# An adding transfer in place of every second low-part subtraction in layer 1's MLP

## The chip, the cores and the metric

The kernel runs on one core of a Trainium2 chip. The metric is the device time of one execution in microseconds; lower is better. Engines are named by their work: TensorE (PE in the profile, PEld for its weight loads), VectorE (DVE), ScalarE (ACT), GpSimd (POOL) and SyncE (SP, which here only issues loads). Transfers run on the core's sixteen DMA engines, whichever engine issues them.

## The reference, cut to what matters

Two encoder layers on 256 tokens of width 2048, in float32. Each layer has attention and then an MLP; only the MLP matters here.

```python
D_MODEL = 2048; SEQ = 256; D_FF = 4 * D_MODEL
for l in range(2):
    ...                                     # modulation, attention, residual
    h = _rmsnorm(x) * (1.0 + sc_m) + sh_m   # (256, 2048)
    y = jnp.square(jax.nn.relu(h @ w_mlp_in[l])) @ w_mlp_out[l]
    x = x + g_m * y
return _rmsnorm(x, final_norm_g)
```

The first product is `h @ w_mlp_in[l]`, 2048 x 8192 weights; the second is the one with `w_mlp_out[l]`, 8192 x 2048.

## The kernel before, in words

**Products in parts.** TensorE multiplies in a shortened format (`F32R`). For float32 accuracy every operand v is split into a high part, v rounded to that format, and a low part, v minus the high part. A product is then three: high by high, high by low and low by high. Where the 256 tokens are the moving operand, one matmul of 512 columns (high and low part of the tokens side by side) takes the weight's high part (line 217), and one of 256 columns the weight's low part (line 220).

**Weights on their way.** `weights(src)` loads one tile of 128 x 2048 float32 (1024 KB) into a buffer of the tag `raw`, of which there are five, by SP's queue (line 170). `part` then makes the parts of each half: ScalarE copies 128 x 1024 into a `hi` buffer (line 151), VectorE subtracts that copy from the raw values into a `lo` buffer (line 154). There are four `hi` and four `lo` buffers, so two tiles' worth. `more_ada` follows, which now and then starts one load for the modulation vectors; in layer 1's MLP it does so seldom (two of these sums are in that stretch).

**Layer 1's MLP.** `block_by_seven` runs four times, once for each 2048 of the 8192 hidden columns (`fb`). A block has 16 tiles of 128 hidden columns; in block 0 the first six are computed by another routine with the norm, so ten are left, and in blocks 1 to 3 all sixteen. Each of these 58 tiles is one call of `wides` with one source: sixteen matmuls with the high parts, one per 128 of the 2048 inputs, then sixteen with the low parts. The first eight of each sixteen read the tile's first half, the last eight its second. So the second half's low part is the last that TensorE reads of a tile. `join` then adds the two token halves of the result (line 1366 on ScalarE, line 1367 on VectorE) and frees the bank.

**Between the tiles.** Two tiles, here called A and B, give one pair of hidden columns. `relu`, `split` and `seven` make from them the operands of seven products with part of the second product's weights (`in_w_ms`, 1024 KB for a pair), in place of eight. `seven` gives two steps that run later, between tiles: `five` (fifteen matmuls, three weight parts: raw 512 wide, raw 1024, combined 1024) behind a tile A and `two` (six matmuls, one combined part) behind a tile B, lines 1170 to 1172. Each of their parts takes a `hi` and a `lo` buffer as well. The steps begin with the fifth tile of a block's loop, so the first tiles of a block follow each other directly. Behind a block's tiles come the remaining quarters of the second product (lines 311, 312 and 314).

**What sets the order.** Each engine works its queue in order. The order is made by a scheduler before the run: by program order as priority, as soon as the operands and a free buffer of the tag are there by its own estimate. A `hi` or `lo` buffer is free again when the last matmul that reads it has ended. GpSimd's queue (POOL) issues only a few transfers: the gate of an MLP or attention block goes to HBM and back spread over all partitions (lines 1277 and 1279), in layer 1's MLP once, behind block 0's tiles.

Of the kernel before, what the change touches and what calls it, by code (L numbers as in the profile page):

```python
# [10 lines left out]
F32R = mybir.dt.float32r  # L11
I32 = mybir.dt.int32
AF = mybir.ActivationFunctionType
ALU = mybir.AluOpType
AX = mybir.AxisListType

P = 128
# [84 lines left out]
class Trunk:  # L102
    def __init__(self, ctx, tc, io):
        self.nc, self.tc, self.io = tc.nc, tc, io
        pool = lambda name, bufs, **k: ctx.enter_context(tc.tile_pool(name=name, bufs=bufs, **k))
        self.cp = pool("cp", 1)
        self.wp = pool("wp", 4)
        self.up = pool("up", 40)
        self.tp = pool("tp", 6)
        self.sp = pool("sp", 8)  # L110
        self.pp = pool("pp", 8, space=bass.MemoryType.PSUM)
        self.dp = pool("dp", 1, space=bass.MemoryType.DRAM)
        self.ada_todo, self.ada_here, self.rate, self.credit = [], [], 0.0, 0.0
        self.sums, self.by_act, self.by_dve = [], [], []
        self.bias_out = None
        self.quiet = False
        self.n = 0

    def name(self, s):
# [14 lines left out]


    def weights(self, src, width=2048, order=None):
        raw = self.raw(src, width)
        half = width // 2
        out = []
        for i in range(2):  # L140
            w, ins = self.part(raw, i, half, order and order[1], order and order[0])
            out.append(w)
        self.more_ada(ins)
        return out

    def part(self, raw, i, half, after=None, hi_after=None):

        v = raw[:, i * half : (i + 1) * half]
        hi = self.wp.tile([P, half], F32R, tag="hi", name=self.name("hi"), bufs=4)
        lo = self.wp.tile([P, half], F32R, tag="lo", name=self.name("lo"), bufs=4)  # L150
        ins = self.nc.scalar.activation(hi, v, AF.Copy)  # L151
        if hi_after is not None:
            self.behind(ins, hi_after)
        ins = self.nc.vector.tensor_tensor(lo, v, hi.bitcast(F32), ALU.subtract)  # L154
        if after is not None:
            self.behind(ins, after)
        return (hi, lo), ins
# [922 lines left out]
    def block_by_seven(self, fb, h, banks):  # L1080

        io = self.io
        hid, steps, sums = [], [], []
        plain = len(banks)
        for m in range(0, plain, 2):
            hid += self.relu2(self.joined(banks[m : m + 2], self.t("sum")))
        for m in range(plain, NK, 2):
            both = self.t("sum")
            for j in range(2):
                ps = self.wides([io["w_m11"][NK * fb + m + j - 6]], h)[0]  # L1090
                self.join(ps, both[:, j])
                if m > plain + 2:
                    steps.pop(0)()
            r = self.relu(both)
            parts = self.split(r, "hid", True)
            hid += parts
            steps += self.seven(io["w_ms"][fb, m // 2], parts, r, sums, m == plain, m == NK - 2)
        for f in steps:
            f()
        if fb == 0:  # L1100
            self.gate(1, 5)
        end = fb == NFB - 1
        done = self.final if end else self.updates
        first, adds, halves = self.four(sums)
        first()
        light = adds + [lambda c=c: done(halves[c], c) for c in range(2)]
        pss = [self.bank("pr") for _ in range(2)]
        for kq in range(4):
            self.rows_by_k(pss, self.weights(io["w_m2"][1, fb, 2, kq]), hid, kq)
            if kq < 3 or not plain:  # L1110
                light.pop(0)()
        done(pss, 2)
        if plain:
            self.both_by_k([self.weights(io["w_ms"][fb, m // 2]) for m in range(0, plain, 2)], hid, halves)
            light.pop(0)()
        if end:
            light.pop(0)()
            pss = self.rows(io["w_m2"][1, fb], hid, 3, True)
        else:
            pss = [self.bank("pr") for _ in range(2)]  # L1120
            for kq in range(4):
                self.rows_by_k(pss, self.weights(io["w_m2"][1, fb, 3, kq]), hid, kq)
                if light:
                    light.pop(0)()
        done(pss, 3)
# [534 lines left out]
```

## Time and profile before

| | |
|---|---|
| median of 3 runs | 2150.16 us (2149.0 to 2150.75) |
| span of the profiled execution | 2147.8 us |
| its own time | no other than the span is given; the median of the runs is 2.36 us above it |
| TensorE busy | 2122.2 us, 99% |
| VectorE busy | 1776.3 us, 83% |
| ScalarE busy | 1209.9 us, 56% |
| GpSimd busy | 6.2 us |
| moved by DMA | 594.76 MB, 277 GB/s over the span |
| layer 1's MLP in the trace | from about 1490 us to the end |

How it is read: the page and the views of the trace come from one profiled execution. The busy times of the engines overlap. A row of the windows gives the busy time and number of instructions of each engine in a stretch, the granted TensorE clock, the DMA engines' mean busy share and their rate. A row of the waits says who waited on which line for whom: total us, times, longest. A row of the chain gives start, duration, engine, tile and line, and how many instructions were merged. A row of a transfer gives the size and the median time from issue to landing.

### The profile page before, as it was taken

What the parts mean: (1) busy time and instruction counts of PE and PEld (TensorE: products, weight loads), DVE (VectorE), ACT (ScalarE), POOL (GpSimd) and SP (SyncE); (2) the same over time, 40 slices, a digit from 0 to 9 for tenths busy, and PEclk for the clock granted to TensorE, in tenths of its full rate; (3) what the DMA queues carried; (4) which work ended last, traced back from release to release, by engine and by line L of the source; (5) the groups of instructions that cost most, each with busy time, mean ns of one, the idle gap of its engine ahead of it and who ended that gap; (6) DMA issues with size and microseconds to landing.
All of it is one profiled execution on the core that took longest, in us unless ns stands there. A gap on an engine that the chain in (4) does not pass through costs nothing.

```text
span 2147.8 us, 29564 instructions
## 1 busy us (share of the span) xinstructions
PE 2122.2 (99%) x11411; PEld 1841.3 (86%) x11411; DVE 1776.3 (83%) x2444; ACT 1209.9 (56%) x1829; POOL 6.2 (0%) x18
## 2 busy tenths in 40 slices
PE   7999999999999999999999999999999999999998
PEld 6899887898888888888889998888888888888886
DVE  8889888988688888888877886778977897897897
ACT  6555663565465355345455576647645765664674
POOL 0000000000000000000000000000000000000000
PEclk9999999999999999999999999999999999999999
DMA  9989899799888888988967776776665564565553
GB/s 395 423 343 334 324 353 346 285 335 344 322 318 329 347 319 323 341 311 318 344 222 275 255 254 236 274 250 210 227 237 186 184 239 153 198 233 177 191 191 128
DMA packets 87245, 594.76 MB, mean 277 GB/s; under 512 B 9856, under 2 KB 10304, under 8 KB 20288
## 3 DMA queue, kind: packets, MB, share of 16 engines
q1 hardware_dynamic: 85536, 586.41, 73.9%
q0 software_dynamic: 848, 5.28, 0.6%
q8 instruction: 89, 1.46, 0.3%
q10 hardware_dynamic: 720, 1.19, 0.2%
q14 instruction: 52, 0.43, 0.1%
HBM read 589.66 MB, written 3.18 MB: 276 GB/s over the span
## 4 chain that ended last, share of the span: by engine, by line
PE 92%; DVE 3%; DMA 2%; ACT 2%; issue 1%; ACTq 0%; DVEq 0%
PE ps L217 19%; PE pr L311 10%; PE pr L314 10%; PE pr L312 10%; PE ps L220 10%; PE pk L260 3%; PE pk L284 2%; PE pk L194 2%; PE pk L198 2%; PE pk L197 2%; PE pp L1171 2%; PE pp L1170 2%; PE pp L1172 2%; PE pv L298 2%; PE pv L296 2%; PE pv L297 2%
## 5 line engine op out<-in xcount | busy, mean ns | idle before, releaser
L151 ACT ACTIVATE hi<-raw 128x1024 fp32r<-128x1024 f32 (+2 forms) x714 | 720.1, 1019 | 617.0 <-PE pr L312 275.6
L154 DVE TENSOR_TENSOR lo<-raw,hi 128x1024 fp32r<-128x1024 f32 (+2 forms) x714 | 821.1, 1171 | 261.8 <-issue 105.5
L380 DVE SCALAR_TENSOR_TENSOR ada<-ada,cond 128x2048 f32<-128x2048 f32 x192 | 438.2, 2284 | 13.8 <-DMA ada<-in_w_ada 13.1
L217 PE MATMUL ps<-h,hi 128*128 128x512 f32 x1856 | 436.5, 390 | 0.0
L217 PEld LDWEIGHTS ps<-h,hi 128*128 128x128 f32 x1856 | 345.2, 188 | 71.1 <-DVE sum L1367 1.3
L311 PE MATMUL pr<-hi,hid 128*128 128x512 f32 x768 | 298.9, 389 | 0.0
L312 PE MATMUL pr<-hi,hid 128*128 128x512 f32 x768 | 298.8, 389 | 0.0
L220 PEld LDWEIGHTS ps<-h,lo 128*128 128x128 f32 x1856 | 234.2, 191 | 6.8
L220 PE MATMUL ps<-h,lo 128*128 128x256 f32 x1856 | 236.2, 283 | 0.0
L314 PE MATMUL pr<-lo,hid 128*128 128x512 f32 x768 | 190.3, 389 | 0.0
L312 PEld LDWEIGHTS pr<-hi,hid 128*128 128x128 f32 x768 | 144.2, 188 | 29.9
L314 PEld LDWEIGHTS pr<-lo,hid 128*128 128x128 f32 x768 | 144.1, 188 | 29.9
L311 PEld LDWEIGHTS pr<-hi,hid 128*128 128x128 f32 x768 | 144.1, 188 | 29.8
L1366 ACT ACTIVATE sum<-ps 128x256 f32<-128x256 f32 x110 | 42.0, 382 | 87.4 <-PE ps L220 86.8
L194 PE MATMUL pk<-h,hi 128*128 128x256 f32 x320 | 90.4, 285 | 0.2 <-ACT h L715 0.2
L198 PE MATMUL pk<-h,lo 128*128 128x256 f32 x320 | 90.5, 283 | 0.0
L197 PE MATMUL pk<-h,hi 128*128 128x256 f32 x320 | 90.5, 283 | 0.0
L260 PE MATMUL pk<-hf,w 128*128 128x256 f32 x384 | 83.9, 379 | 0.0
L260 PEld LDWEIGHTS pk<-hf,w 128*128 128x128 f32 x384 | 72.8, 190 | 9.9
L154 DVE TENSOR_TENSOR lo<-comb,hi 128x1024 fp32r<-128x1024 f32 x58 | 70.4, 1218 | 6.3 <-PE ps L220 6.3
L151 ACT ACTIVATE hi<-comb 128x1024 fp32r<-128x1024 f32 x58 | 60.7, 1052 | 8.5 <-PE pp L1172 5.5
L194 PEld LDWEIGHTS pk<-h,hi 128*128 128x128 f32 x320 | 61.2, 192 | 0.6 <-ACT h L715 0.5
(288 smaller groups left out, 3129.2 us busy)
## 6 DMA issues: line engine op xcount, KB each, us to landing
raw<-in_w_m SPq DMA_DIRECT2D x206, 1024.0 KB, 5.9
ada<-in_w_ada SPq DMA_DIRECT2D x192, 1024.0 KB, 6.5
raw<-in_w_o SPq DMA_DIRECT2D x32, 1024.0 KB, 5.7
raw<-in_w_ms SPq DMA_DIRECT2D x32, 1024.0 KB, 5.0
raw<-in_w_m SPq DMA_DIRECT2D x24, 768.0 KB, 5.4
raw<-in_w_dv SPq DMA_DIRECT2D x16, 1024.0 KB, 5.8
raw<-in_w_t SPq DMA_DIRECT2D x12, 1024.0 KB, 5.0
w<-in_w_a SPq DMA_DIRECT2D x24, 384.0 KB, 13.5
```

Source lines behind the costliest of these rows:

```text
L151: ins = self.nc.scalar.activation(hi, v, AF.Copy)
L154: ins = self.nc.vector.tensor_tensor(lo, v, hi.bitcast(F32), ALU.subtract)
L194: ins = mm(ps, hi, x[0], start=first, stop=False, skip_group_check=shared)
L197: mm(ps, hi, x[1], start=False, stop=False, skip_group_check=shared)
L198: self.last_mac = mm(ps, lo, x[0], start=False, stop=last, skip_group_check=shared)
L217: mm(ps.rearrange("p a b -> p (a b)"), part(w, k, 0), x[2], start=k == 0, stop=False)
L220: mm(ps[:, 0], part(w, k, 1), x[0], start=False, stop=k == nk - 1)
L260: self.nc.tensor.matmul(ps, v, whole[k], start=first, stop=last, skip_group_check=True)
L311: mm(ps, xh[:, c], part(i, 0), start=kq == 0 and i == 0, stop=False)
L312: mm(ps, xl[:, c], part(i, 0), start=False, stop=False)
L314: self.last_mm = mm(ps, xh[:, c], part(i, 1), start=False, stop=kq == 3 and i == 3)
L380: ins = nc.vector.scalar_tensor_tensor(w, w, 1.0, self.cond, ALU.mult, ALU.mult, accum_out=acc[:, i : i + 1])
```

## The change

For the 58 tiles, the second half's low part is no longer made by VectorE. ScalarE writes the negated, rounded copy of the raw values (scale -1) into the `lo` buffer, and GpSimd's queue issues a transfer that reads the same half of the tile a second time from HBM (128 x 1024 float32, 512 KB) and adds it to what stands in the buffer, so that v minus the high part results. ScalarE makes the `hi` copy of that half as before. The first half goes through `part` unchanged, now after the second: the second half takes its `hi` and `lo` buffers first. TensorE's order of products is the same. The number of buffers, the loads by SP and everything else are as before.

```diff
@@ class Trunk, __init__
         self.quiet = False
+        self.adding = False
         self.n = 0
@@ weights
     def weights(self, src, width=2048, order=None):
+        if self.adding:
+            return self.weights_by_adding(src, width)
         raw = self.raw(src, width)
...
+    def weights_by_adding(self, src, width):
+
+        raw = self.raw(src, width)
+        half = width // 2
+        tile = lambda tag: self.wp.tile([P, half], F32R, tag=tag, name=self.name(tag), bufs=4)
+        hi, lo = tile("hi"), tile("lo")
+        v = raw[:, half:]
+        self.nc.scalar.activation(lo, v, AF.Copy, scale=-1.0)
+        self.nc.gpsimd.dma_start(lo, src[:, half:], accum_op=ALU.add)
+        self.nc.scalar.activation(hi, v, AF.Copy)
+        w, ins = self.part(raw, 0, half)
+        self.more_ada(ins)
+        return [w, (hi, lo)]
@@ block_by_seven
             for j in range(2):
+                self.adding = True
                 ps = self.wides([io["w_m11"][NK * fb + m + j - 6]], h)[0]
+                self.adding = False
                 self.join(ps, both[:, j])
```

## The prediction

> **What bounds the kernel now.** First the head of the page, then the table of windows over layer 1's MLP: block 0 with its output product, two whole blocks' worth, the last with the end, and three of the steady pairs and back-to-back tiles inside it.
>
> ```profile
> span 2147.8 us, 29564 instructions
> PE 2122.2 (99%) x11411; PEld 1841.3 (86%) x11411; DVE 1776.3 (83%) x2444; ACT 1209.9 (56%) x1829; POOL 6.2 (0%) x18
> ```
> ```profile
> core 0: us, PE busy (x) PEld busy (x) DVE busy (x) ACT busy (x) POOL busy (x), PEclk, DMA share, GB/s
> 1490.00:1606.00 116.00, 115.95 (x578) 98.20 (x577) 101.83 (x144) 72.21 (x98) 1.05 (x2) 1.00 0.62 227
> 1606.00:1806.00 200.00, 199.59 (x1011) 169.47 (x1010) 165.40 (x223) 115.70 (x149) 0.00 (x0) 1.00 0.54 192
> 1806.00:1976.00 170.00, 169.59 (x860) 143.87 (x858) 144.13 (x199) 103.42 (x136) 0.00 (x0) 1.00 0.55 196
> 1976.00:2147.80 171.80, 163.04 (x827) 138.08 (x825) 142.79 (x205) 105.15 (x151) 0.00 (x0) 0.98 0.48 172
> 1693.50:1709.40 15.90, 15.90 (x87) 13.79 (x86) 14.16 (x21) 11.02 (x16) 0.00 (x0) 1.00 0.56 196
> 1623.20:1645.40 22.20, 22.20 (x130) 19.64 (x129) 17.38 (x26) 11.35 (x16) 0.00 (x0) 1.00 0.36 116
> ```
>
> From 1490 to 1976 us TensorE is idle for 0.05 + 0.41 + 0.41 = 0.87 us, at full clock. The 8.8 us without matmuls in the last window lie at the very end, behind the last product. VectorE, which the change relieves, is 89% busy in a steady pair (14.16 of 15.90) and bounds nothing there. A busy TensorE can still be late inside a stretch, so the waits of its weight loads and matmuls over the same stretch come next:
>
> ```profile
> PEld pp L1171 <- DVE lo L154: 3.2, 7, 0.6
> PEld pp L1170 <- ACT sh L1161: 2.4, 4, 0.7
> PEld ps L217 <- DVE sum L1367: 1.3, 6, 0.3
> PEld pp L1172 <- DVE sl L1162: 0.5, 3, 0.2
> PE pp L1170 <- ACT sh L1161: 0.7, 3, 0.2
> PE pp L1171 <- DVE lo L154: 0.5, 3, 0.2
> ```
>
> All that any engine makes TensorE wait in layer 1's MLP is 8.6 us: 5.5 for VectorE (3.2 + 0.5 + 1.3 + 0.5) and 3.1 for ScalarE. A weight load also runs ahead of its matmul, so part of this costs nothing. The most that a lighter VectorE can bring is therefore 5.5 us, 0.26% of the time. The span is 2.4 us below the median of the runs, 2150.16; I add that 2.4 to what I work out on the span.
>
> **The change, part by part.** It touches the 58 tiles of the first product that call `wides` one at a time (10 in block 0, 16 in each of the others).
>
> *VectorE* loses one 128x1024 low part per tile, *ScalarE* gains one negating copy of the same size:
>
> ```profile
> L154 DVE TENSOR_TENSOR lo<-comb,hi 128x1024 fp32r<-128x1024 f32 x58 | 70.4, 1218 | 6.3 <-PE ps L220 6.3
> L151 ACT ACTIVATE hi<-raw 128x1024 fp32r<-128x1024 f32 x5 | 5.3, 1060 | 1.7 <-PE ps L217 1.1 <-PE pp L1172 0.6
> ```
>
> VectorE: 58 x 1.22 = 71 us less in total, per pair 14.16 - 2.44 = 11.7 of 15.90. ScalarE: 58 x 1.06 = 61 us more, per pair 11.02 + 2.12 = 13.1 of 15.90; in the run of four back-to-back tiles 11.35 + 4 x 1.06 = 15.6 of 22.2. Both stay below TensorE's time, so neither becomes the bound by its sum. What ScalarE loses is slack: 4.9 us free per pair become 2.8. Where it is densest, at the first pair of each of the four blocks, the copy pushes the products that wait for `sh` (the 3.1 us above) later. Bounds: none of it, or 2 x 1.06 per block = 8.5 us. I take 2 us, near the lower end, since a copy has to fit into 2.8 us of idle. Against it stand the 5.5 us of waits for VectorE; bounds 0 and 5.5, I take 2, since loads run ahead. These two cancel.
>
> *GpSimd and SP.* 58 issues on POOL's queue, which holds only 1.05 us of work in block 0 and none afterwards in the table. Its two transfers of the gate start at 1559.65 and 1564.82, in block 0's output product, when that block's adding transfers are over and the next block's are not yet due; nothing queues behind them:
>
> ```profile
> 1559.65 0.50 POOL L1277 DMA_DIRECT2D gate<-modT  x1 [202.37 <-ACT modT L1276]
> 1564.82 0.55 POOL L1279 DMA_DIRECT2D bias<-gate  x1 [4.68 <-DVE lo L154]
> ```
>
> 58 x 0.55 = 32 us of POOL time hides in an empty queue. SP's loads are the same in number. A `raw` buffer is now let go by two ScalarE copies and one low part, not later than now, because the second read of the weights comes from HBM. I cost both at nothing; the cover is POOL's empty queue, and if one issue took more than half a pair (8 us) it would be gone.
>
> *The transfer, and the wait that it adds.* This is the term that decides. TensorE's last eight products of a tile read the low half that ScalarE fills with the negated high half and the DMA completes. Today that half is ready 1.2 us after its high half. The question is whether it lands before TensorE is there. The chain, in order of time, for one pair (L217: sixteen high products, L220: sixteen low ones; between tiles the products of `seven`):
>
> ```profile
> 1661.89 3.68 PE ps L217 x16
> 1665.57 1.91 PE ps L220 x16
> 1670.69 3.63 PE ps L217 x16
> 1674.31 1.91 PE ps L220 x16
> 1677.61 3.75 PE ps L217 x16
> 1681.37 1.91 PE ps L220 x16
> ```
>
> Low buffers are four, taken in turn. A pair takes eight: tile A two, `five` three, tile B two, `two` one. With the second half's pair now taken first, B's second half gets the buffer of A's first half, and the next A's second half that of the last part of `five`.
> Tile B: A's first low half is read out at 1665.57 + 0.96 = 1666.5. The negation ends at 1667.6, if ScalarE is free. B reads the result from 1674.31 + 0.96 = 1675.3. The transfer has 7.7 us, or 6.6 if ScalarE comes one copy late.
> Next tile A: the buffer is free when `five` ends, 1670.69; with one other copy first the negation ends at 1672.8; needed at 1681.37 + 0.96 = 1682.3: 9.5 us.
> Tiles back to back at a block's start: the buffer is free at the end of tile n and needed by n+2 a whole tile (5.6 us) and 3.63 + 0.96 later: 10.2 - 1.1 = 9.1 us.
> Tile B is the tight one: 6 of them in each of blocks 1 to 3 and 3 in block 0, 21 in all.
>
> How long does an adding transfer of 512 KB take? The trace has none. The nearest rows:
>
> ```profile
> bias<-bias_kept POOLq DMA_DIRECT2D x1, 1024.0 KB, 5.1
> bias<-gate POOLq DMA_DIRECT2D x4, 1024.0 KB, 8.1
> raw<-in_w_ms SPq DMA_DIRECT2D x32, 1024.0 KB, 5.0
> out_y<-x SPq DMA_DIRECT2D x6, 256.0 KB, 2.1
> w<-in_w_d SPq DMA_DIRECT2D x6, 512.0 KB, 14.8
> DMA to landing us min/median/max: 4.7/5.0/8.6
> ```
>
> From below 2.1 us (256 KB, plain); from above 8.6 (the slowest of the `in_w_ms` loads, the last row) and, far off, 14.8 (512 KB in the crowded start of layer 0). An adding transfer has to read both the weights and what stands in the buffer, 2 x 512 KB, so I take POOL's plain 1024 KB load from HBM, 5.1 us, and 0.4 for the handover from ScalarE to POOL: an estimate of 5.5 us. That is 2.2 us inside the tightest slack: nothing on the path. At 8.6 + 0.4 = 9.0 tile B would be late by 1.3 us, and at 14.8 by about 7.
>
> A rule of the Trainium skill bears on this term. "Collectives: The Full Stack", section "The bandwidth ceiling: the fold count and why AG ≠ RS ≠ AR", says that the sum in a DMA costs nothing itself, but that reading two sources for one written halves the rate, from about 31 to 16 GB/s an engine. By it 512 KB on 16 engines are an estimated 2.1 us of moving, behind a fixed part that is below the 2.1 us of the 256 KB row: some 4.2 us in all, an estimate, and the sum stays 2150. By the rows alone it was 5.5 us and the same sum. No run here shows the rule yet.
>
> *DMA load.*
>
> ```profile
> 1671.09 1.46 SPq L170 DMA_DIRECT2D raw<-in_w_m  x2
> ```
>
> A pair moves three 1024 KB loads at a share of 0.56: 0.56 x 15.90 / 3 = 3.0 us of all sixteen engines per load. Two adding transfers add 2 x 1.5 (one read) to 2 x 3.0 (two reads): a share of 0.75 to 0.93. Below 1, so hidden, with little to spare at the upper end.
>
> **Sum:** 2147.8 + 2 (ScalarE) - 2 (VectorE) + 0 (POOL, SP) + 0 (transfer, load) = 2147.8 on the span; with 2.4 beside it 2150.2. Predicted 2150.
>
> **The rivals.**
> *The transfer is late (ends slower).* Place: the ninth low product of tile B. Point from which it decides: 7.7 us from the end of the negation to the landing. Price: 21 x the excess; at 9.0 us 21 x 1.3 = 27 us, 2177; with ScalarE one copy late (6.6) 21 x 2.4 = 50, 2200; at 14.8 about 21 x 7 = 150 and some 45 more for the back-to-back tiles, 2345. For it: nothing in the trace shows that the adding form moves at the plain rate, and two loads are issued in the middle of the pair, at 1671.09. Against it: the 5.1 us row. Chance 0.27.
> *The DMA engines fill.* If an adding transfer takes more than (15.90 - 0.56 x 15.90) / 2 = 3.5 us of all engines, a pair lasts as long as its DMA: at 4.5 us 0.56 x 15.90 + 9.0 = 17.9, 2 us more on 29 pairs, 58 us, 2208. For it: the share of 0.93 at two reads. Against it: 3.0 is already two full reads at the rate of the loads. Chance 0.08. The Trainium skill's "DMA: Bandwidth & Descriptors", section "Issuing engines are not separate DMA queues", is on its side: transfers from POOL and SP interleave on the same sixteen engines, so POOL brings no room of its own; the trace of before has no moment with both to test it.
> *ScalarE becomes late.* In order, with 2.8 us free per pair, it delays `sh` and the next tile's high halves; at its upper bound 8.5 us, less 2 from VectorE: 2157. For it: ScalarE already makes TensorE wait 3.1 us. Against it: 82% busy at most. Chance 0.10.
> *VectorE's waits vanish and nothing takes their place (faster).* All 5.5 us: 2145. Against it: ScalarE is loaded in the same places. Chance 0.07.
>
> **How the numbers follow.** Forecast 0.48, rivals 0.27, 0.08, 0.10, 0.07. About 0.2% (4.3 us) can be told from no change. Slower: 0.27 + 0.08 + 0.07 of ScalarE's 0.10 = 0.42. The same: 0.48 + 0.03 = 0.51. Faster: 0.07, only the whole of the 5.5 us. The likeliest case alone lies in 2146 to 2154. The range goes from 2145 (all VectorE waits gone) to 2195: it holds the late transfer up to about 2.1 us on each tile B, and leaves out what is later still and a DMA that fills, about 0.18.
>
> **What would show it.** Right: `lo` from ScalarE x58 at 1.06 us and the low parts of `raw` on VectorE 58 fewer; an adding transfer that lands within 7.7 us; no wait of TensorE for a DMA at L220; pairs of 15.9 us; a DMA share of 0.75 to 0.93. Wrong: a wait of L220's weight loads for the adding transfer (how long, and in which tiles: B alone, or all), pairs longer than 16 us, a share at 1, or waits of L1170 for `sh` that have grown from 3.1 us. The forecast rests most on the 5.1 us row standing for a transfer of another kind.

## The result, and the profile after

The changed kernel takes 2222.21 us (median of 4 runs, 2218.62 to 2227.28) against 2150.27 for the kernel before: a ratio of 1.0337, interval 1.0321 to 1.0352, 72 us slower. It lies above the range of 2145 to 2195. The mechanism that the prediction priced under its first rival (the transfer is late) is part of it, but in more tiles than named there, and with two costs beside it.

The profiled execution took 2224.25 us, its span 2222.5, 74.7 more than before. First, from the page, its head and two rows of the transfers (size, median us from issue to landing):

```profile
span 2222.5 us, 29750 instructions
...
PE 2145.5 (97%) x11411; PEld 1851.7 (83%) x11411; DVE 1714.0 (77%) x2386; ACT 1257.7 (57%) x1887; POOL 56.9 (3%) x76
...
raw<-in_w_ms SPq DMA_DIRECT2D x32, 1024.0 KB, 8.5
lo<-in_w_m POOLq DMA_DIRECT2D x58, 512.0 KB, 8.0
```

The work moved as worked out: 58 instructions fewer on VectorE, 58 more on ScalarE, as many matmuls as before. TensorE is nevertheless 23 us longer busy. The adding transfer takes 8.0 us in the median, not 5.5, and the `in_w_ms` loads went from 5.0 to 8.5 us. Now the waits in layer 1's MLP (who on which line for whom: total us, times, longest):

```profile
DVE comb L1198 <- DMA raw<-in_w_ms: 53.3, 18, 4.9
...
PEld ps L237 <- DMA lo<-in_w_m: 42.7, 26, 5.7
...
PE ps L237 <- DMA lo<-in_w_m: 37.3, 24, 5.5
...
PEld pp L1190 <- DVE lo L171: 15.4, 16, 2.0
...
PE pp L1190 <- DVE lo L171: 9.6, 10, 1.6
...
PEld ps L234 <- ACT hi L168: 3.4, 5, 0.8
```

Lines 234, 237 and 1190 are 217, 220 and 1171 of the kernel before. Two waits are new or grown: TensorE waits for the adding transfer (37.3 us of idle array in 24 places), and `seven`'s low parts on VectorE come late (9.6 us of idle array, 0.5 before) because VectorE now waits 53.3 us for the raw `in_w_ms` loads. The windows, in the columns of before: the whole MLP up to the last product, and three stretches around one late transfer.

```profile
1490.00:2210.00 720.00, 670.12 (x3257) 558.68 (x3256) 491.43 (x705) 439.81 (x583) 49.93 (x58) 0.98 0.72 216
1869.00:1873.60 4.60, 4.60 (x25) 3.90 (x24) 2.88 (x7) 4.36 (x7) 0.00 (x0) 1.00 0.99 294
1873.60:1877.00 3.40, 0.27 (x4) 0.07 (x2) 0.00 (x0) 0.92 (x2) 0.00 (x0) 1.00 0.79 272
1877.00:1881.70 4.70, 4.70 (x18) 3.92 (x19) 4.09 (x5) 2.58 (x4) 0.45 (x1) 0.64 0.02 3
```

TensorE is idle 720.00 - 670.12 = 49.9 us, where it was idle for about 1 us. The mean share of the DMA engines, 0.72, is a little below what was forecast (0.75 to 0.93), but the share jumps between 0.99 and 0.02. And behind the stall of the third row the granted clock falls to 0.64 over the fourth. The timeline of that tile (start, duration, engine, line, operation):

```profile
1862.89 2.06 SPq L187 DMA_DIRECT2D raw<-in_w_m  x2
...
1865.20 0.87 POOL L157 DMA_DIRECT2D lo<-in_w_m  x1 [5.44 <-ACT lo L156]
...
1867.98 0.33 SPq L187 DMA_DIRECT2D raw<-in_w_ms  x1
...
1869.05 3.86 PE L234 MATMUL ps<-h,hi 128*128 128x512 f32 x16
...
1872.75 1.11 PE L237 MATMUL ps<-h,lo 128*128 128x256 f32 x8
...
1876.99 1.22 PE L237 MATMUL ps<-h,lo 128*128 128x256 f32 x8 [3.13 <-DMA lo<-in_w_m]
...
1878.28 0.63 PE L1191 MATMUL pp<-hi,hid 128*128 128x512 f32 x1
```

Two 1024 KB loads start within the 2.3 us before the adding transfer and a third 2.8 us behind it. The transfer is issued at 1865.20 and TensorE's ninth low product, due at 1873.86 (8.7 us later; the prediction counted 9.5 for a tile A, from the end of the negation), starts at 1876.99, 11.8 us after the issue. Directly behind it a matmul of 512 columns takes 0.63 us in place of 0.40, and the next ones start every 0.43 us in place of 0.23: the granted clock is at half speed for 3.4 us.

In the granted-clock records of the MLP, up to the last product, there are eight such episodes, 34.1 us long in all; at half speed that is 17 us of work lost. 49.9 us of idle array less about 1 before, and 17, are 66 of the 74.7 us. The other 9 were not attributed one by one; weight loads that come late for less than the work ahead of them are a likely place, which no run tests.

### The profile page after: what moved, and what is told of

Its sections match the earlier page's. It is cut to its first block, busy times and chain, and to the rows that moved or that the text cites. A ratio compares the mean times of both kernels' runs of the same rounds, so it can differ in the third digit from the quotient of the medians.

```text
span 2222.5 us, 29750 instructions
## 1 busy us (share of the span) xinstructions
PE 2145.5 (97%) x11411; PEld 1851.7 (83%) x11411; DVE 1714.0 (77%) x2386; ACT 1257.7 (57%) x1887; POOL 56.9 (3%) x76
## 5 line engine op out<-in xcount | busy, mean ns | idle before, releaser
L171 DVE TENSOR_TENSOR lo<-raw,hi 128x1024 fp32r<-128x1024 f32 (+2 forms) x656 | 752.3, 1167 | 323.2 <-ACT hi L168 144.5
L168 ACT ACTIVATE hi<-raw 128x1024 fp32r<-128x1024 f32 (+2 forms) x656 | 657.6, 1014 | 552.7 <-PE pr L329 245.6
L397 DVE SCALAR_TENSOR_TENSOR ada<-ada,cond 128x2048 f32<-128x2048 f32 x192 | 438.1, 2284 | 13.1 <-DMA ada<-in_w_ada 12.0
L237 PE MATMUL ps<-h,lo 128*128 128x256 f32 x1856 | 245.9, 286 | 37.4 <-DMA lo<-in_w_m 37.3
L158 ACT ACTIVATE hi<-raw 128x1024 fp32r<-128x1024 f32 x58 | 61.4, 1059 | 38.0 <-PE ps L234 14.6
L1198 DVE TENSOR_TENSOR comb<-raw 128x1024 f32<-128x1024 f32 x29 | 35.5, 1223 | 53.4 <-DMA raw<-in_w_ms 53.3
```

What stands on the lines that cost most here:

```text
L237: mm(ps[:, 0], part(w, k, 1), x[0], start=False, stop=k == nk - 1)
L397: ins = nc.vector.scalar_tensor_tensor(w, w, 1.0, self.cond, ALU.mult, ALU.mult, accum_out=acc[:, i : i + 1])
```

## The experiments

Two theories stood against each other at first: the moment (the transfer is issued too late for the tile that needs it, in certain tiles), and the load (the transfers and SP's loads slow each other, wherever they are issued). Each run below is given with the ratio to the kernel before, timed in turns on the same chip, and its 95% interval.

**The halves swapped, and ScalarE's copy, without a transfer.** First the order of the halves alone, with VectorE making both low parts; then the change without its transfer (the low half stays the negated high half).

```diff
+        hi, lo = tile("hi"), tile("lo")
+        self.nc.scalar.activation(hi, v, AF.Copy)
+        self.nc.vector.tensor_tensor(lo, v, hi.bitcast(F32), ALU.subtract)
+        w, ins = self.part(raw, 0, half)
```

> The kernel before with one thing of the change: in the 58 tiles the second half takes its buffers and is converted first; no negated copy, no adding transfer, VectorE makes both low parts. It splits the small loss that stays without the transfer (about 5 us at the median): if the order of the halves is what costs, 2154 to 2157; if ScalarE's further copies do, 2149 to 2152.

2150.05 us, 1.0000 (0.9991 to 1.0008): the order of the halves costs nothing.

```diff
         self.nc.scalar.activation(lo, v, AF.Copy, scale=-1.0)
-        self.nc.gpsimd.dma_start(lo, src[:, half:], accum_op=ALU.add)
```

> The changed kernel without the adding transfer: ScalarE writes the negated copy, TensorE reads it as the low part (the second half's low part is therefore left uncomputed). Theory 'collision' (the transfer alone lands in about 5.7 us and in time; SP's loads that run beside it stretch it to 10 to 12 us, and it makes theirs late): the whole loss goes, 2147 to 2154. Theory 'adding' (the adding form itself is what is expensive): the same, 2147 to 2154. Theory 'schedule' (ScalarE's 58 further copies and the new order of buffers make the tiles late): most of the loss stays, 2190 or more.

2156.45 us (2151.63 to 2158.07), 1.0023 (1.0012 to 1.0034), a little above the 2147 to 2154 of two of the theories. VectorE's 71 us less bring nothing that is seen; ScalarE's 58 copies cost about 5 us net. That is a small part of the 72: the rest came with the transfer.

**A plain transfer in place of the adding one.** It reads the weights only, not what stands in the buffer (the low half then holds the weights themselves).

```diff
-        self.nc.gpsimd.dma_start(lo, src[:, half:], accum_op=ALU.add)
+        self.nc.gpsimd.dma_start(lo, src[:, half:])
```

> POOL issues a plain transfer of the same 512 KB into the low buffer in place of the adding one, behind the same negated copy (the low part is therefore the raw value). Same bytes from HBM, same waits, no read of the destination. Engine time per transfer by the loads' row 1.5 us in place of the 3.1 us that the trace of the changed kernel gives. 'Collision': it lands sooner (about 4 us alone, 6 to 8 beside loads), few waits stay, 2152 to 2185. 'Adding': it lands in 4 us nearly always, 2148 to 2155. 'Schedule': 2190 or more.

2174.93 us, 1.0109 (1.0094 to 1.0124). Its transfers and loads, and its waits in the MLP:

```profile
raw<-in_w_ms SPq DMA_DIRECT2D x32, 1024.0 KB, 7.5
lo<-in_w_m POOLq DMA_DIRECT2D x58, 512.0 KB, 4.3
```
```profile
DVE comb L1198 <- DMA raw<-in_w_ms: 34.9, 17, 4.3
...
PE pp L1190 <- DVE lo L171: 12.6, 11, 1.9
...
PEld ps L237 <- DMA lo<-in_w_m: 3.1, 4, 1.3
```

At 4.3 us the transfer is hardly ever late (3.1 us), and still the kernel loses 24 us: `in_w_ms` lands late, VectorE's combinations with it, and TensorE waits for them (12.6 us of idle array, 0.5 before). So the loads' lateness is a cost of its own, and one that the prediction had at nothing. The other 47 us of the change come with the adding form.

**The addend from the raw buffer instead of HBM.** The same sum, but no second read of the weights from HBM.

```diff
-        self.nc.gpsimd.dma_start(lo, src[:, half:], accum_op=ALU.add)
+        self.nc.gpsimd.dma_start(lo, v, accum_op=ALU.add)
```

> The adding transfer takes its addend from the raw buffer in SBUF, not a second time from HBM. The same reads for the DMA engines, 30 MB less from HBM; the raw buffer is held until the transfer has read it, so SP's next loads start later. 'Collision' on the sixteen engines: the transfer takes as long as before (5.7 alone, 10 to 12 beside loads), 2200 to 2245. If HBM is what is contended: 2150 to 2185. 'Adding': near 2222.

2196.78 us (2193.72 to 2208.22), 1.0223 (1.0195 to 1.0251). The transfer takes 4.4 us at least, 5.3 in the median and 12.4 at most, 14 of 58 over 9 us, and TensorE's weight loads wait for it 30.6 us. The profiled execution was the slowest of the four, 2208.22 us. The array idles 27.3 us for the transfer, where it was 37.3 in the change: without the second read from HBM most of that wait is still there, so HBM's bandwidth is not the main cause. The total, about two thirds of the loss, says less, since this run adds a cost of its own: the transfer holds the `raw` buffer that it reads, and VectorE's combinations wait 20.4 us for it.

**The transfers beside the work.** In blocks 1 to 3 the same copies and transfers run, but into a buffer that nobody reads there, and VectorE makes the low half as before. No matmul of these blocks waits for a transfer.

```diff
+        junk = lo if self.side is None else self.cond[:, half * self.side : half * self.side + half].bitcast(F32R)
+        self.nc.scalar.activation(junk, v, AF.Copy, scale=-1.0)
+        self.nc.gpsimd.dma_start(junk, src[:, half:], accum_op=ALU.add)
...
+            self.nc.vector.tensor_tensor(lo, v, hi.bitcast(F32), ALU.subtract)
```

> In blocks 1 to 3 the negated copy and the adding transfer go into a buffer that nobody reads (two halves in turn), and VectorE makes the low part as before the change; block 0 (10 tiles) stays changed. The DMA engines carry the same, TensorE waits for no adding transfer there. 'Collision': the loads of in_w_ms are still late (8 us rather than 5), TensorE still waits for VectorE's parts of them, but the direct waits (37 of the 50 us) go: 2155 to 2185. 'Adding', where only the wait for the result costs: 2150 to 2160, no late loads. 'Schedule': 2190 or more.

2176.77 us, 1.0120 (1.0105 to 1.0135), 26 us. What TensorE waits for here is VectorE's late `seven` parts (14.4 us of weight loads), the sums (6.6) and, in block 0 alone, the transfer (5.7); `in_w_ms` takes 7.1 us. Of the 18 us of idle array, 5 lie in block 0, and half clock follows the longest stall there. So transfers that nobody waits for cost less than 26 us, at most about a third of the change; VectorE, which in blocks 1 to 3 is not relieved in this run, has its part in that.

**In which tiles.** Three runs make the change in one kind of tile each: the back-to-back tiles at a block's start (16), the tiles A (21) and the tiles B (21).

```diff
-                self.adding = True
+                self.adding = m <= plain + 2              # back to back
...
+                self.adding = j == 0 and m > plain + 2    # A
...
+                self.adding = j == 1 and m > plain + 2    # B
```

> The change in the first four tiles of each block alone (16 of 58), which follow each other with nothing between them; few loads run there (DMA share 0.36 before the change). 'Collision': most transfers land in 5.5 to 7.5 us, in time, 2147 to 2158. 'Adding' or 'schedule', by which each tile costs alike: 16/58 of 72, so 2170.

> The change in 21 tiles alone: those called A, from the fifth tile of a block on. Their transfer is issued just when SP starts two loads of 1024 KB. 'Collision' with SP's loads: it still takes 9 to 11 us and is late, 2170 to 2195. If it was the transfer of the tile B before it, 4 us earlier, that stretched it: it lands in 7 us or less, 2150 to 2160. An equal cost per tile: 21/58 of 72, 2176.

> The change in the 21 tiles called B alone, behind the fifteen products of five, the ones with the least slack by my count (7.7 us, about 6 from the issue). Their transfer mostly runs where no load does. 'Collision': 5.5 to 6.5 us, just in time, 2148 to 2165. 'Schedule' (issued too late behind ScalarE's join): late by 1 to 2 us on each, 2170 to 2190. An equal cost per tile: 2176.

Back to back: 2152.49 us, 1.0006 (0.9996 to 1.0015). A: 2179.87, 1.0136 (1.0120 to 1.0152). B: 2194.34 (2179.20 to 2202.79), 1.0196 (1.0148 to 1.0244). B alone lost more than any of its three expectations allowed. The three losses, 2 + 30 + 44 = 76 us, add up to about the whole 72 (B's interval is wide, 32 to 52 us). The back-to-back tiles are as safe as the prediction had them; tile A is not. One tile A, from the timeline of the run with A alone:

```profile
1696.13 1.46 SPq L187 DMA_DIRECT2D raw<-in_w_m  x2
...
1698.07 0.86 POOL L157 DMA_DIRECT2D lo<-in_w_m  x1 [15.06 <-ACT lo L156]
...
1702.72 3.82 PE L234 MATMUL ps<-h,hi 128*128 128x512 f32 x16
...
1706.38 1.11 PE L237 MATMUL ps<-h,lo 128*128 128x256 f32 x8
...
1709.47 1.22 PE L237 MATMUL ps<-h,lo 128*128 128x256 f32 x8 [1.98 <-DMA lo<-in_w_m]
```

From the issue to the ninth low product there are 1707.49 - 1698.07 = 9.4 us, just as counted (9.5 from the negation). But the two loads started 2 and about 1 us earlier share the engines, and the product comes 11.4 us after the issue. In this run the transfer takes 7.4 us at the least and 9.3 in the median. Now one tile B, from the run with B alone:

```profile
1720.36 2.08 PE L237 MATMUL ps<-h,lo 128*128 128x256 f32 x16
...
1722.47 0.38 ACT L1385 ACTIVATE sum<-ps 128x256 f32<-128x256 f32 x1 [0.33 <-PE ps L237]
...
1722.93 1.06 ACT L168 ACTIVATE hi<-raw 128x1024 fp32r<-128x1024 f32 x1
...
1723.90 1.04 ACT L156 ACTIVATE lo<-raw 128x1024 fp32r<-128x1024 f32 x1
...
1725.24 0.86 POOL L157 DMA_DIRECT2D lo<-in_w_m  x1 [20.42 <-ACT lo L156]
...
1725.64 0.33 SPq L187 DMA_DIRECT2D raw<-in_w_m  x1
...
1727.34 0.33 SPq L187 DMA_DIRECT2D raw<-in_w_ms  x1
...
1729.10 1.11 PE L237 MATMUL ps<-h,lo 128*128 128x256 f32 x8
...
1735.46 2.08 PE L237 MATMUL ps<-h,lo 128*128 128x256 f32 x8 [5.26 <-DMA lo<-in_w_m]
```

The buffer is free at 1721.4, after eight of the sixteen low products of tile A. But ScalarE's queue has the join of tile A (line 1385, which waits for all sixteen) and another high half ahead of the negation, so this ends at 1724.94, not at 1722.5. From the issue to the need are 5.0 us. Then a load starts 0.4 us after the transfer, another 2.1 us after, and the transfer takes 10.2 us instead of 5.5: 5.3 us of idle array. Four of the 21 tiles B have this shape and wait 5.3 us each, 21 of the 26.8 us that the array idles for the transfer in this run; twelve transfers land in 5.4 to 5.7 us and make TensorE wait for 0.2 us at most; in each of these the next load starts at least 1.6 us behind the issue.

**Fewer loads.** The 29 `in_w_ms` loads are left out; VectorE combines from a buffer that is there already.

```diff
-            raw = self.raw(src, 2048)
+            raw = self.cond
```

> The changed kernel with the 29 loads of 1024 KB for five and two left out: their weights are taken from a buffer that stands there anyway (so these products are left uncomputed). A third of the loads of a pair goes, and the raw buffers are freer. 'Collision': DMA share from 0.72 to about 0.5, transfers 6 to 9 us, no late comb, 2150 to 2180. 'Adding' and 'schedule': 2205 or more, since the transfer and ScalarE's work are the same.

2160.44 us, 1.0048 (1.0033 to 1.0063): 10 us in place of 72, with all 58 adding transfers in it. The median transfer takes 6.8 us (8 over 9 us), the weight loads wait 11.1 us for it, and VectorE's lateness is gone with the loads. So the change needs the loads beside it to be dear: neither the copies nor the transfers by themselves make it so. (With the loads left out `raw` buffers are free earlier too; the run does not separate the two.)

**A longer lead.** Two buffers of its own for the second half's low part in blocks 1 to 3, so that the negation need not wait for the rotation of `lo`:

```diff
+            lo = self.own[:, half * self.side : half * self.side + half]
```

> The changed kernel, but in blocks 1 to 3 the low part of a tile's second half has two buffers of its own (A and B in turn), so the negated copy waits for no other part's buffer. Program order is the same. If lateness was the buffer's (as my count of the slack had it): copies move some 4 us ahead for A, waits mostly go, 2155 to 2180. If the place in ScalarE's queue (behind the join of tile A) and SP's loads set it: nothing moves for B, 2195 to 2225.

2195.56 us, 1.0217 (1.0204 to 1.0231). This did not give a clear answer. The waits for the transfer fell to 7.2 (own buffers) and 6.4 us (block 0), but a new one came up, of TensorE for ScalarE's high halves, 22.5 us where it was 3.4. With other buffers ScalarE's queue has another order, and the negation, no longer held by a buffer, now waits there 30.9 us for the raw load; the high halves that stand behind it are held up with it. In the next run the raw load, the negation and the transfer of a tile are all issued one tile ahead, before the present tile's join:

```diff
+    def make_ready(self, src, side):
+        raw = self.raw(src, 2048)
+        lo = self.own[:, 1024 * side : 1024 * side + 1024]
+        self.nc.scalar.activation(lo, raw[:, 1024:], AF.Copy, scale=-1.0)
+        self.nc.gpsimd.dma_start(lo, src[:, 1024:], accum_op=ALU.add)
+        self.ready.append((raw, lo))
...
                 ps = self.wides([io["w_m11"][NK * fb + m + j - 6]], h)[0]
+                if fb and m + j < NK - 1:
+                    self.make_ready(io["w_m11"][NK * fb + m + j - 5], 1 - j)
```

> As own_low, and in blocks 1 to 3 the load, the negated copy and the adding transfer of the next tile stand in the program ahead of the present tile's join, so ScalarE does the copy before it. Transfers and bytes are the same 58. If the transfer is late for want of a few us of lead: issued 3 us or more earlier for B, waits for the adding transfer under 10 us, 2155 to 2175 (late loads of in_w_ms still cost some). If the DMA engines' load is the cause whatever the lead: 2195 or more.

2170.94 us (2166.09 to 2178.22), 1.0100 (1.0083 to 1.0116). In the profile, of the slowest execution, the waits that are left stand where the lead is short: 6.4 us in block 0, which has the old order, and 10.5 us in four tiles at the start of blocks, where tiles follow each other directly and three of the four transfers take over 11 us. So the last run keeps the early issue and adds only in the 36 tiles of blocks 1 to 3 from the fifth on:

```diff
-                self.adding = True
+                self.adding = fb > 0 and m >= 4
...
-                if fb and m + j < NK - 1:
+                if fb and 3 <= m + j < NK - 1:
```

> As own_early, but only in the 36 tiles of blocks 1 to 3 from the fifth on, where five and two run between the tiles; block 0 and the first four tiles of a block are as before the change. If a lead of 8 us or more from the issue to the tile's start is all that the transfer lacked: no wait for it, pairs of 15.9 us, 2147 to 2153. If transfers beside the loads cost something whatever the lead: 36/58 of what own_early lost, 2160 or more.

2149.65 us (2148.42 to 2152.59), 0.9997 (0.9988 to 1.0006). The waits of TensorE's loads in the MLP that are over 1 us, one tile of the timeline from its transfer to its last eight products, and two windows:

```profile
PEld pp L1209 <- DVE lo L185: 2.4, 7, 0.7
...
PEld pp L1208 <- ACT sh L1199: 1.6, 4, 0.4
PEld ps L248 <- ACT hi L182: 1.3, 2, 1.0
```
```profile
1881.39 0.88 POOL L155 DMA_DIRECT2D own<-in_w_m  x1 [7.67 <-PE pp L1210]
...
1889.91 3.79 PE L248 MATMUL ps<-h,hi 128*128 128x512 f32 x16
...
1894.49 1.12 PE L251 MATMUL ps<-h,own 128*128 128x256 f32 x8
```
```profile
1806.00:1976.00 170.00, 170.00 (x865) 145.14 (x864) 131.80 (x187) 111.95 (x149) 10.48 (x12) 1.00 0.77 234
1881.10:1897.00 15.90, 15.90 (x87) 13.79 (x86) 12.10 (x19) 12.35 (x18) 1.75 (x2) 1.00 0.87 252
```

No wait for the transfer is left. Issued 8.5 us before its tile and 13.1 before the tile's last eight products, it costs nothing: a pair lasts 15.90 us at full clock, as before, at a DMA share of 0.87. It also wins nothing, though VectorE is relieved in 36 tiles. The moment decides, and where the moment is right, the load is carried. Two things changed with the moment, and this run does not separate them: the lead is at least 12.4 us, about as long as the slowest transfer of the changed kernel (12.7), and the transfers are now issued further from SP's loads and land sooner, in 5.7 us in the median and 9.7 at most.

## Why the prediction was wrong, point by point

*What bounds the kernel, and the most there is to win: right.* TensorE was busy all the time, and relieving VectorE won nothing that can be measured: by 71 us in the run without transfers, by 36 x 1.22 = 44 us in the last one. The cap of 5.5 us was even generous: it adds waits of the array to the waits of its weight loads for the same parts, and the array itself idled for only 1.3 us from 1490 us to the last product.

*VectorE and ScalarE, -2 and +2: near in size, but not by the mechanism.* Without the transfer it was 5.4 us slower, inside the bounds of 0 to 8.5 for the copies, and that is luck. In its profiled execution (span 2151.2) the waits for ScalarE did not grow; those for VectorE did, to 11 us in place of 5.5, and VectorE's combinations waited 10.7 us for `in_w_ms` in place of 1.6. So the copies seem to let the `raw` buffers go later, against the prediction's sentence on them; no run tests that by itself.

*GpSimd's queue: right.* An issue took 0.87 us where 0.55 was taken, 49.93 us in all, in an otherwise empty queue.

*The transfer by itself: right, or nearly.* 5.1 us from issue to landing and 0.4 for the handover were taken; undisturbed it takes 5.4 to 5.8, behind a handover of about 0.3. Of DMA time the upper end was the right one, from the queues in the changed kernel's MLP and then in the plain run's:

```profile
q0 software_dynamic: 8292, 30.57, 23.6%
```
```profile
q0 software_dynamic: 8240, 30.42, 14.9%
```

Over stretches of 732 and 670 us with 56 transfers that is 0.236 x 732 / 56 = 3.1 us of all sixteen engines for an adding transfer and 0.149 x 670 / 56 = 1.8 for a plain one (a little of it the gate's); 3.0 and 1.5 were worked out. The Trainium skill's rule that two sources read halve the rate ("Collectives: The Full Stack", section "The bandwidth ceiling: the fold count and why AG ≠ RS ≠ AR") agrees with this ratio of 1.7, roughly; the 4.2 us that the prediction drew from it were too low, as no adding transfer from HBM landed in under 5.3.

*"The transfer, and the wait that it adds" is the step that failed*, in three ways.
First, a duration on undisturbed engines was set against the slack. All 58 transfers meet at least one load before they land, and it matters when that starts: in 36 a load was issued between 2.5 us before the transfer's issue and 1.0 us behind it, and 24 of these took over 9 us, up to 12.7; the other 22 took 5.5 to 7.1. The prediction had quoted the two loads issued in the middle of a pair, but put them under a rival. The trace of before had an example, too, in the prediction's own row `bias<-gate`, 8.1 us. It stands for four POOL transfers of 1024 KB; their times from issue to landing, and the window of the last one, with the DMA engines full (share 1.01, 423 GB/s):

```profile
DMA to landing us min/median/max: 5.1/8.1/8.9
```
```profile
1564.82:1572.98 8.16, 8.16 (x37) 6.76 (x36) 8.16 (x11) 3.64 (x4) 0.55 (x1) 1.00 1.01 423
```

In the three of 8.0 to 8.9 us a load of SP had been issued 0.4 to 0.6 us earlier; in the one of 5.1 us none had for 5.8 us. The sum used a 5.1. A busy VectorE is not what stretches the transfers of the change: in the 5 us behind their issue it was busy for 77% beside those under 7 us and 51% beside those over 9.

Tile A, called safe at 9.5 us, had about the slack that was counted and was 0 to 3 us late for this alone.

Second, tile B's slack was counted from the moment when the buffer is free. On ScalarE the negation stood behind the join of tile A, and at times behind another high half. From the end of the negation 5.3 us were left in the tile shown (5.0 from the issue), not 7.7 or 6.6. An undisturbed 5.5 us from the issue would have been late by half a microsecond there, and would have fitted into the 5.6 to 6.9 us of sixteen other tiles B of that run; so this decides together with the first.
Third, what follows a wait was costed at nothing. A stall of TensorE brought half clock behind it: 17 us in the profiled execution. That price was in no term.

*"SP's loads ... at nothing" failed too.* Their number is the same, but they slow as the adding transfers do: `in_w_ms` 5.0 to 8.5 us. Through VectorE's combinations this makes TensorE late: 9.6 us of idle array here, and 12.6 of the 17.8 us of idle array with the plain transfer.

*"DMA load": the mean was about right, the conclusion not.* 0.75 to 0.93 was forecast for a pair, 0.72 measured over a longer stretch. A mean below 1 does not hide a transfer that comes due within a few microseconds, while the share around it is 0.99. Nor did the engines fill, as the second rival had it: the run with the long lead carries 0.87 at full speed. The Trainium skill's "DMA: Bandwidth & Descriptors", section "Issuing engines are not separate DMA queues", says that transfers from different engines interleave on the same sixteen. The prediction held that the trace of before has no moment with both; it has at least three, the slow `bias<-gate` transfers above, and these runs show it in both directions (5.5 to 12.7 us, and 5.0 to 8.5).

*The first rival* had the right place for part of it (tile B) and gave 27 us at 9.0 us of landing, or 50 with ScalarE a copy late. B alone cost 44. That the 50 comes near is luck: it is 2.4 us in each of 21 tiles, and in the run with B alone four tiles wait 5.3 us each, the others 6 together, and half clock behind them takes some 15 more.

What stays open: how the late loads and the late transfers split the loss of the tiles A, since each makes the other late; and whether the longer lead or the quieter place made the early transfers free.

## What to carry to other kernels

Take the duration of a transfer from where it will run, beside the loads that its own stretch issues, and count the slack from its issue as the queues have it, not from when the buffer is free. A mean DMA share below 1 says that the transfers fit in, not that each lands in time: 36 of these transfers, issued 13 us before their need instead of mostly 6 to 10, cost nothing. And before paying for a relief, see whether the relieved engine ever set the pace: here it did not, and up to 71 us less work on VectorE was worth nothing.

## What the runs showed of the hardware that was not expected

**The clock falls behind a short stall.** The stall of 5.3 us in the tile B shown above, and a window behind it, in the run with B alone:

```profile
1730.20:1735.46 5.26, 0.01 (x1) 0.00 (x0) 1.23 (x1) 0.00 (x0) 0.00 (x0) 0.89 1.00 306
1735.46:1738.90 3.44, 3.44 (x12) 3.15 (x13) 1.27 (x3) 0.59 (x2) 0.00 (x0) 0.50 0.03 12
```

The clock stays at half speed for 6.8 us in all. Shorter stalls did it too, but not always, and the granted-clock records show which. In each run all episodes begin on one grid of 3.413 us (their starts modulo 3.413 agree within 0.002 us), and what counts is how long the array idles within one window of that grid. Such windows, from the run with the plain transfer and then from the run with A alone:

```profile
1849.79:1853.21 3.42, 1.50 (x7) 0.96 (x6) 3.42 (x5) 2.43 (x3) 0.53 (x1) 1.00 0.13 14
1853.21:1856.62 3.41, 3.41 (x9) 2.62 (x9) 3.19 (x4) 1.68 (x2) 0.00 (x0) 0.50 0.81 228
```
```profile
1885.35:1888.76 3.41, 2.25 (x14) 1.84 (x12) 2.53 (x8) 2.73 (x4) 0.00 (x0) 1.00 1.02 335
1888.76:1892.17 3.41, 2.07 (x13) 1.90 (x14) 1.54 (x4) 0.73 (x2) 0.00 (x0) 1.00 0.15 61
1892.17:1895.59 3.42, 3.42 (x17) 2.83 (x16) 3.42 (x5) 2.81 (x4) 0.00 (x0) 1.00 0.16 22
```

A stall of 1.9 us within one window was followed by half clock; one of 2.5 us that fell into two windows (1.16 and 1.34 us) was not. In the nine runs with such episodes in layer 1's MLP, 35 windows at full clock were followed by half clock, and the least idle of them idled for 1.72 us; 1727 were not, and the most idle of those idled for 1.81. So the limit lies at about half of a window. An episode lasts 3.41 us, or 6.83 where the array idled in its first half as well (0.67 us or more; up to 0.48 us did not prolong it). The Trainium skill, "TensorE: Matmul & The Clock Gate", section "Part 1: The HAM clock gate (the "warmup" mystery)", has a free-running window of 3413 ns and half rate after at least one idle window of about 3.4 us. The window, its fixed grid and the half rate agree; but here a window idle for about half of its time was enough.

**Nearly half of the engine time of an adding transfer comes with the adding:** 1.8 us without it, 3.1 with it, and in the change the difference between 24 and 72 us. Whether that is the read of the destination or the sum, no run here separates.
